# A hybrid layer on one core: rounded parts of x kept in DRAM between two sweeps, gates written as tanh, two transposes issued together, gates placed later

## The chip, the cores and the metric

One Trainium2 chip, one of its cores. The metric is the device time of one execution in microseconds (us), as the median of several runs. The core has five engines that work beside each other: PE (TensorE, matrix products), DVE (VectorE), ACT (ScalarE, functions from tables), POOL (GpSimd) and SP (SyncE, which here does nothing but issue DMAs). Each takes its instructions in its own order and waits on semaphores for the others.

## The reference

The function is one layer over a prompt of 2048 tokens and 8 decode sequences of 4 tokens, with model width 1024. Cut to what matters here:

```python
xn = rms_norm(x, g_mix_norm)
h  = xn @ w_in                        # widths: pool 256, rnn 512 + gate 512, attention 256
xc = causal_dwconv(rnn part)          # 4 taps
r  = sigmoid(xc @ w_rg_a + b_rg_a)    # 8 blocks of 64 x 64
i  = sigmoid(xc @ w_rg_x + b_rg_x)
log_a = -8 * r * softplus(-lam);  a = exp(log_a)
bt = sqrt(-expm1(2 * log_a)) * i * xc
h_t = a_t * h_{t-1} + bt_t            # scan over tokens
rnn_out = h * gelu(gate part)
pool_out: trailing means over 2, 4, 8, 16 tokens, minus the token, times w_pool
attn_out: cross attention, 4 heads of 64, over 256 memory rows (decode: its own cached k and v)
x = x + concat(group rms of the three) @ w_out
x = x + (gelu(conv3(xn2 @ w_ff_gate)) * (xn2 @ w_ff_up)) @ w_ff_down
y = rms_norm(x, g_final)
```

## The kernel before

Tokens stand on the columns, channels on the 128 partitions. The 2080 columns are cut into six slices s = 0 to 5 of 344 or 348 columns; slice 0 holds the 32 decode columns. All matrix products of the projections are made in rounded float32: an operand z is split into a high part, rounded by ACT, and a low part, z minus the high part, made by DVE (`split_g` does it for x with the norm's gain, L127 and L128), and a product is the sum of three matmuls (high times high, low times high, high times low). The two parts of two of x's eight chunks lie in a pair of tiles (`ahr`, `alr` in sweep 1, `ahp`, `alp` in sweep 2).

- Sweep 1 (0 to about 251 us of the profile) makes the recurrent branch. For each slice, `proj2` makes four groups of 48 matmuls: `pr` twice (the recurrent input) and `pq` twice (the gate input). DVE multiplies by the row norms (xr, L520; g, L549), ACT and DVE make the convolution (xc, L529 and L532), the block matrices give the gates (`g_gates`: pg on PE, L452; sigmoids on ACT, L455; the factor on DVE, L458), then ACT makes tanh (L466), exp (L469), the square (L470) and a square root (L472), which with DVE's L471 and L473 give the scan's input; L559 scans, L576 multiplies with gelu's result (L556).
- Then the keys and values of the memory, and sweep 2 (from about 263 us): the columns' x is loaded and split a second time (`xp`), and the pool and query projections (`pf` for slice 0, then `pq`), attention and pool are made. In the decode part, `pTd` holds two transposes of the softmax's result, L736, and `wz` its copies, L739; `pVd` (L745) multiplies with the cached values.
- Then the output projection, and three blocks of the feed-forward part (from about 525 us to the end).

What sets the order: PE and SP take their instructions in the order of the program's text. `Weave` holds generators (a norm, the gates, the preparation of the next slice) which are advanced between the matmuls of `proj2` when an estimated clock has passed their due time; the table `W` holds those waits. ACT, DVE and POOL are ordered by a scheduler when the program is built. A weight `w` is loaded to one of three staging tiles (`st_wr`) and split to `h_wr` and `l_wr` (L122, L123); the order of SP's loads decides when that starts. ACT loads a table of functions when the next function is not in the one it has (ACT_TABLE_LOAD).

Of the kernel before, what the change touches and what calls it, by code (L numbers as in the profile page):

```python
# [43 lines left out]
def hybrid_kernel(ctx: ExitStack, tc: tile.TileContext, I, O):  # L44
# [71 lines left out]
    def pcol(name, j):  # L116
        return pv[:, PC[name] + j:PC[name] + j + 1]


    def split(hi, lo, src, eng=None):  # L120

        S.activation(out=hi, in_=src, func=AF.Copy)  # L122
        (eng or V).tensor_tensor(out=lo, in0=src, in1=hi.bitcast(F32), op=ALU.subtract)  # L123

    def split_g(hi, lo, src, g):

        S.activation(out=hi, in_=src, func=AF.Copy, scale=g)  # L127
        V.scalar_tensor_tensor(out=lo, in0=src, scalar=g, in1=hi.bitcast(F32), op0=ALU.mult, op1=ALU.subtract)  # L128
# [106 lines left out]
    def half(h):  # L235
        return slice(64 * (h % 2), 64 * (h % 2) + 64)
# [4 lines left out]
    def psC(name):  # L241
        return ps.tile([P, 512], F32, tag="C", bufs=4, name=name)

    def g_prep(st, src, n, g, name, parts=2, wait=1.2, pool=0):

        x = big([P, 8, n], "x" + name)
        st += [x, [pair(f"{name}{k}", n) for k in range(KD // 2)]]
        w = KD // parts
        for k in range(KD):
            if k == 0 or (parts > 2 and k % w == 0):  # L250
                for h in range(k, k + w if parts > 2 else KD, w):
                    nc.sync.dma_start(out=x[:, h:h + w, :], in_=src[:, h:h + w, :])
            hi, lo = (z[:, k % 2, :] for z in st[1][k // 2])
            if k % 2 and k // 2 < pool:
                S.activation(out=x[:, k, :], in_=x[:, k, :], func=AF.Copy, scale=pcol(g, k))
                split(hi, lo, x[:, k, :], G)
            else:
                split_g(hi, lo, x[:, k, :], pcol(g, k))
# [186 lines left out]
    def g_gates(s, c2, n, st):  # L445

        xc, r, ii = st["xc"], st["r"], st["i"]
        dec = s == 0
        for c in (2 * c2, 2 * c2 + 1):
            pg = [psC(f"pg{s}{c}{h}") for h in range(2)]  # L450
            for h in range(2):
                T.matmul(pg[h][:, 0:n], bdg[half(h), c, :], xc[half(h), c, :], start=True, stop=True)  # L452
            for d, (dst, bias) in enumerate(((r, "ba"), (ii, "bx"))):
                for h in range(2):
                    S.activation(out=dst[half(h), c, :], in_=pg[h][half(d ^ h), 0:n], func=AF.Sigmoid,  # L455
                                 bias=pcol(bias, c)[half(h)])
            if c % 2:
                V.tensor_tensor(out=ii[:, c - 1:c + 1, :], in0=ii[:, c - 1:c + 1, :], in1=xc[:, c - 1:c + 1, :],  # L458
                                op=ALU.mult)
            yield 0.6, W["g2"]  # L460
        if c2 == 1:
            th = xc
            a2 = big([P, 4, n], f"a2{s}")

            for c in range(4):
                S.activation(out=th[:, c, :], in_=r[:, c, :], func=AF.Tanh, scale=sc8[:, c:c + 1])  # L466
            a = st["a"] = r
            for c in range(4):
                S.activation(out=a[:, c, :], in_=r[:, c, :], func=AF.Exp, scale=nl[:, c:c + 1])  # L469
            S.activation(out=a2, in_=a, func=AF.Square)  # L470
            V.scalar_tensor_tensor(out=th, in0=a2, scalar=1.0, in1=th, op0=ALU.add, op1=ALU.mult)  # L471
            S.activation(out=th, in_=th, func=AF.Sqrt)  # L472
            V.tensor_tensor(out=ii, in0=ii, in1=th, op=ALU.mult)  # L473
            if dec:
                d0 = kp.tile([P, 4, NB], F32, name="d0")
                V.tensor_tensor(out=d0, in0=t0(a), in1=h0, op=ALU.mult)
                V.tensor_tensor(out=t0(ii), in0=t0(ii), in1=d0, op=ALU.add)
                V.memset(t0(a), 0.0)

    for s in range(NS):  # L480
# [73 lines left out]
        while "a" not in st:
            wv.tick(0.5)
        S.activation(out=g, in_=g, func=AF.Gelu_apprx_tanh)  # L556
# [78 lines left out]
    def g_attn(s, n, npr, p0, qd, qs):  # L635
# [25 lines left out]
        def transp(j):  # L661
            e, c0, w = es[j]
            e_done.append(e)
            for mc in range(2):
                pT = psC(f"pT{s}{j}{mc}")
                for h in range(4):
                    T.transpose(pT[:, h * w:(h + 1) * w], e[:w, h, mc * P:(mc + 1) * P], ident[:w, :w])
                pv4 = pT[:, 0:4 * w].rearrange("p (h t) -> p h t", h=4)
                if mc >= W["n_pt"]:
                    S.activation(out=PT[:, mc, :, c0:c0 + w], in_=pv4, func=AF.Copy)  # L670
                else:
                    V.tensor_copy(PT[:, mc, :, c0:c0 + w], pv4)
# [33 lines left out]
    def g_dec(qd, ox):  # L706
# [27 lines left out]
        pT = psC("pTd")  # L734
        for mc in range(2):
            T.transpose(pT[:, mc * P:(mc + 1) * P], e[:, 0, mc * P:(mc + 1) * P], ident)  # L736
            pt4 = pT[:, mc * P:(mc + 1) * P].rearrange("p (g b m) -> p g b m", g=4, b=2)
            for b2 in range(2):
                V.tensor_copy(wf[:, mc, :, b2, 16 * b2:16 * b2 + 16], pt4[:, :, b2])  # L739
# [20 lines left out]
    for s in range(NS):  # L760
# [3 lines left out]
        p0 = ND if dec else 0  # L764
        npr = n - p0
        if s:
            wv.finish(pg_)
            x = xq.pop(s)
        rb = RBP.pop(s)
        if s + 1 < NS:  # L770
            xq[s + 1] = []
            pg_ = g_prep(xq[s + 1], x_src(s + 1), NCOL[s + 1], "g_mix", f"p{s + 1}", 2, W["prep_p"], W["n_prep"])
            wv.add(pg_)
            wv.tick(0.0)
        if s + 1 < NS:
            wv.add(g_bcast(rsx[:, s + 1, :], NCOL[s + 1], *TOK[s + 1], new_rbp(s + 1), f"p{s + 1}"), 0.0 if dec else W["bc_p"])
            wv.tick(0.0)
# [840 lines left out]
```

## Time and profile before

| | |
|---|---|
| median of 3 runs | 2127.59 us (2126.03 to 2129.19) |
| profiled execution | 2129.87 us, span 2128.0 us |
| PE busy | 2065.4 us, 97% |
| DVE busy | 1633.5 us, 77% |
| ACT busy | 1323.1 us, 62% |
| HBM read, written | 289.17 MB, 122.92 MB |

The span is what the trace covers; the execution's own time is 1.9 us more. A wait row names the waiting engine and tile, then the engine, tile and line whose end it waited for. A timeline row is start, duration, engine, line, operation, output from input, and in brackets how long the engine stood idle before. Where PE is at its full clock, a matmul of 348 columns follows the one before after 0.158 us; at half clock after about 0.29 us.

### The profile page before, as it was taken

To read this page: it belongs to the slowest core of one execution; us is meant where nothing else is said; L and a number is where in the kernel's file an instruction comes from. 1 tells how busy PE (TensorE), PEld (TensorE's weight loads), DVE (VectorE), ACT (ScalarE), POOL (GpSimd) and SP (SyncE) were. 2 spreads that over 40 slices of the span, in tenths; PEclk is the share of its full clock that TensorE was granted. 3 is DMA by queue.
4 is the path that set the end of the run, shared out by engine and by line. 5 is a ranking of instruction groups with operands and counts; after the bars stand their busy time and mean duration, and the time that the engine had idled before them with its cause. 6 is when DMAs were issued, how large, how long until landed. Compare 5 with 4: busy or idle time off the path is not lost.

```text
span 2128.0 us, 35270 instructions
## 1 busy us (share of the span) xinstructions
PE 2065.4 (97%) x12996; PEld 2009.0 (94%) x12996; DVE 1633.5 (77%) x2846; ACT 1323.1 (62%) x2380; POOL 69.3 (3%) x82
## 2 busy tenths in 40 slices
PE   8999998998999999999999999999999999999997
PEld 7888887888999999999999999999999999999997
DVE  7886897874878988889888666668778666668774
ACT  7879954552566656566655665557666665557663
POOL 0000000000000000000000000000000000000001
PEclk9999999999999999999999999999999999999998
DMA  4112342235997656677997555677887554677882
GB/s 144 55 55 90 126 169 85 66 111 199 286 305 232 229 194 217 197 242 219 260 262 230 188 187 162 211 261 223 245 248 186 190 191 158 217 261 221 247 226 86
DMA packets 257804, 408.72 MB, mean 192 GB/s; under 512 B 24416, under 2 KB 123456, under 8 KB 257632
## 3 DMA queue, kind: packets, MB, share of 16 engines
q1 hardware_dynamic: 242640, 367.19, 52.7%
q0 software_dynamic: 13760, 37.77, 8.4%
q8 instruction: 102, 1.67, 0.3%
q10 hardware_dynamic: 1232, 1.51, 0.2%
q14 instruction: 70, 0.57, 0.1%
HBM read 289.17 MB, written 122.92 MB: 194 GB/s over the span
## 4 chain that ended last, share of the span: by engine, by line
PE 80%; DVE 7%; ACT 5%; DMA 5%; issue 2%; SPq 0%; POOL 0%; POOLq 0%; DVEq 0%; ACTq 0%
PE bu L1054 9%; PE bg L1054 9%; PE bd L1054 9%; PE ag L1054 6%; PE cg L1054 6%; PE ad L1054 6%; PE cu L1054 6%; PE au L1054 6%; PE cd L1054 6%; PE pq L227 3%; PE po L227 2%; PE pu L227 2%; PE pr L227 1%; PE pf L227 1%; ACT r L455 1%
## 5 line engine op out<-in xcount | busy, mean ns | idle before, releaser
L1158 DVE SCALAR_TENSOR_TENSOR cv<-gt,pv,cv 128x696 f32<-128x696 f32 (+2 forms) x144 | 133.0, 924 | 34.9 <-ACT cv L1153 34.9
L1174 DVE TENSOR_TENSOR u<-u,cv 128x696 f32<-128x696 f32 (+1 forms) x72 | 63.3, 879 | 62.7 <-ACT cv L1170 62.7
L1220 POOL DMA_DIRECT2D ys<-cd x32 | 35.0, 1138 | 1367.2 <-ACT cd L1083 894.1
L1054 PE MATMUL bd<-h4s,wt4d 128*128 128x348 f32 (+1 forms) x288 | 72.8, 326 | 4.2 <-DVE cd L1076 4.2
L1054 PE MATMUL ag<-h5s,wt5g 128*128 128x348 f32 (+1 forms) x288 | 74.8, 322 | 0.0
L1054 PE MATMUL bg<-h4s,wt4g 128*128 128x348 f32 (+1 forms) x288 | 74.6, 322 | 0.0
L1054 PE MATMUL bg<-h1s,wt1g 128*128 128x348 f32 (+1 forms) x288 | 74.5, 322 | 0.0
L1054 PE MATMUL bg<-h3s,wt3g 128*128 128x348 f32 (+1 forms) x288 | 74.5, 322 | 0.0
L1054 PE MATMUL cu<-h6s,wt6u 128*128 128x348 f32 (+1 forms) x288 | 74.5, 321 | 0.0
L1054 PE MATMUL ag<-h0s,wt0g 128*128 128x348 f32 (+1 forms) x288 | 74.5, 321 | 0.0
L1054 PE MATMUL cg<-h6s,wt6g 128*128 128x348 f32 (+1 forms) x288 | 74.5, 321 | 0.0
L1054 PE MATMUL bu<-h4s,wt4u 128*128 128x348 f32 (+1 forms) x288 | 74.4, 321 | 0.1
L1054 PE MATMUL cg<-h2s,wt2g 128*128 128x348 f32 (+1 forms) x288 | 74.4, 321 | 0.0
L1054 PE MATMUL au<-h5s,wt5u 128*128 128x348 f32 (+1 forms) x288 | 74.4, 320 | 0.0
L1054 PE MATMUL au<-h0s,wt0u 128*128 128x348 f32 (+1 forms) x288 | 74.4, 320 | 0.0
L1054 PE MATMUL cu<-h2s,wt2u 128*128 128x348 f32 (+1 forms) x288 | 74.4, 320 | 0.0
L1054 PE MATMUL bu<-h1s,wt1u 128*128 128x348 f32 (+1 forms) x288 | 74.3, 321 | 0.0
L1054 PE MATMUL bu<-h3s,wt3u 128*128 128x348 f32 (+1 forms) x288 | 74.3, 321 | 0.0
L1054 PE MATMUL bd<-h3s,wt3d 128*128 128x348 f32 (+1 forms) x288 | 71.9, 322 | 2.1 <-ACT t6d L1072 2.1
L1054 PE MATMUL cd<-h6s,wt6d 128*128 128x348 f32 (+1 forms) x288 | 73.4, 326 | 0.0
L227 PE MATMUL pr<-ahr,h_wr 128*128 128x348 f32 (+1 forms) x192 | 64.8, 338 | 8.5 <-ACT ahr L127 8.5
L1054 PE MATMUL ad<-h0s,wt0d 128*128 128x348 f32 (+1 forms) x288 | 71.5, 321 | 0.0
(552 smaller groups left out, 7549.3 us busy)
## 6 DMA issues: line engine op xcount, KB each, us to landing
hs<-u SPq DMA_DIRECT2D x24, 696.0 KB, 4.1
ys<-cd POOLq DMA_DIRECT2D x20, 696.0 KB, 11.3
wr22g<-in_w_gate_dram SPq DMA_DIRECT2D x36, 256.0 KB, 4.1
wr11g<-in_w_gate_dram SPq DMA_DIRECT2D x36, 256.0 KB, 4.6
wr12g<-in_w_gate_dram SPq DMA_DIRECT2D x36, 256.0 KB, 4.7
wr22u<-in_w_up_dram SPq DMA_DIRECT2D x36, 256.0 KB, 6.5
wr11u<-in_w_up_dram SPq DMA_DIRECT2D x36, 256.0 KB, 6.6
wr12u<-in_w_up_dram SPq DMA_DIRECT2D x36, 256.0 KB, 6.2
```

The lines of the kernel that those rows point to most:

```text
L227: T.matmul(o, w_[:, ks], z, start=(k == 0 and i == 0), stop=(k == nk - 1 and i == 2))
L455: S.activation(out=dst[half(h), c, :], in_=pg[h][half(d ^ h), 0:n], func=AF.Sigmoid, bias=pcol(bias, c)[half(h)])
L1054: T.matmul(pt[:, 0:n], w[:, w_, ks_(k)], blk.hl[i][a_][:, k, :], start=(i in (0, 2) and k == m == 0), stop=(k == 3 and m == 2), skip_group ...
L1158: V.scalar_tensor_tensor(out=cv[:, z0:nn], in0=gt[:, z0 + t:nn + t], scalar=pcol("fcw", 3 * f + t), in1=cv[:, z0:nn], op0=ALU.mult, op1=AL ...
L1174: V.tensor_tensor(out=u, in0=u, in1=k["cv"][:, i, 0:nn], op=ALU.mult)
L1220: at[N + 14 + 1 + s].append(lambda j=2 * d + s, k=ks[s]: G.dma_start(out=flat(ys[b][j]), in_=qv(k["c"], n), accum_op=ALU.add, max_dma_last ...
```

## The change

Four edits, and the removal of some settings that were zero:

1. `g_prep` gets `keep`. After each odd chunk of x in sweep 1, SP stores the high and the low tile of the pair (128 x 688 or 696) to a DRAM buffer `xhl[s]`, eight DMAs a slice. In sweep 2 `load_parts(s)` loads the eight tiles, in place of the load of x and the eight ACT and eight DVE splits a slice.
2. The sigmoids are written as 0.5 (1 + tanh(0.5 z)): ACT uses Tanh with scale 0.5 and a halved bias `gb`; the factors of a half go into DVE's product with (i + 1), into scale and bias of the tanh and exp behind, and into the root's scale of 0.25.
3. Both transposes of `pTd` are issued ahead of the copies of `wz`.
4. `W["gate"]` goes from 6.8 to 8.2 and `W["g2"]` from 0 to 1.4, so the gates' matmuls stand later between those of the projections.

```diff
-    W = dict(... gate=6.8, ... g2=0)
+    W = dict(... gate=8.2, ... g2=1.4)
...
+    xhl = [dr.tile([P, 2, 8, n], F32, name=f"xhl{s}") for s, n in enumerate(NCOL)]
...
-    def g_prep(st, src, n, g, name, parts=2, wait=1.2, pool=0):
+    def g_prep(st, src, n, g, name, parts=2, wait=1.2, keep=None):
...
+            split_g(hi, lo, x[:, k, :], pcol(g, k))
+            if k % 2 and keep is not None:
+                for i in range(2):
+                    nc.sync.dma_start(out=keep[:, i, k - 1:k + 1], in_=st[1][k // 2][i].bitcast(F32))
             yield 0.0, wait
+
+    def load_parts(s):
+
+        x = [pair(f"p{s}{k}", NCOL[s]) for k in range(KD // 2)]
+        for k in range(KD // 2):
+            for i in range(2):
+                nc.sync.dma_start(out=x[k][i].bitcast(F32), in_=xhl[s][:, i, 2 * k:2 * k + 2])
+        return [None, x]
...
-    for k, _ in enumerate(g_prep(xq[0], x_src(0), NCOL[0], "g_mix", "r0", 4)):
+    for k, _ in enumerate(g_prep(xq[0], x_src(0), NCOL[0], "g_mix", "r0", 4, keep=xhl[0])):
...
-                    S.activation(out=dst[half(h), c, :], in_=pg[h][half(d ^ h), 0:n], func=AF.Sigmoid,
-                                 bias=pcol(bias, c)[half(h)])
+                    S.activation(out=dst[half(h), c, :], in_=pg[h][half(d ^ h), 0:n], func=AF.Tanh, scale=0.5,
+                                 bias=gb[half(h), bias + c:bias + c + 1])
...
-                V.tensor_tensor(out=ii[:, c - 1:c + 1, :], in0=ii[:, c - 1:c + 1, :], in1=xc[:, c - 1:c + 1, :],
-                                op=ALU.mult)
+                V.scalar_tensor_tensor(out=ii[:, c - 1:c + 1, :], in0=ii[:, c - 1:c + 1, :], scalar=1.0,
+                                       in1=xc[:, c - 1:c + 1, :], op0=ALU.add, op1=ALU.mult)
...
-                S.activation(out=th[:, c, :], in_=r[:, c, :], func=AF.Tanh, scale=sc8[:, c:c + 1])
+                S.activation(out=th[:, c, :], in_=r[:, c, :], func=AF.Tanh, scale=sc8[:, c:c + 1],
+                             bias=sc8[:, c:c + 1])
...
-            S.activation(out=th, in_=th, func=AF.Sqrt)
+            S.activation(out=th, in_=th, func=AF.Sqrt, scale=0.25)
...
-            pg_ = g_prep(xq[s + 1], x_src(s + 1), NCOL[s + 1], "g_mix", f"r{s + 1}", 2, W["prep_r"])
+            pg_ = g_prep(xq[s + 1], x_src(s + 1), NCOL[s + 1], "g_mix", f"r{s + 1}", 2, W["prep_r"], xhl[s + 1])
...
-            gp = g_prep(xp, x_src(0), NCOL[0], "g_mix", "p0", 2)
...
-    for _ in gp:
-        pass
-    x = xp
+    x = load_parts(0)
...
         for mc in range(2):
             T.transpose(pT[:, mc * P:(mc + 1) * P], e[:, 0, mc * P:(mc + 1) * P], ident)
+        for mc in range(2):
             pt4 = pT[:, mc * P:(mc + 1) * P].rearrange("p (g b m) -> p g b m", g=4, b=2)
...
-            xq[s + 1] = []
-            pg_ = g_prep(xq[s + 1], x_src(s + 1), NCOL[s + 1], "g_mix", f"p{s + 1}", 2, W["prep_p"], W["n_prep"])
-            wv.add(pg_)
-            wv.tick(0.0)
+            xq[s + 1] = load_parts(s + 1)
```

SP at the start of the program, before. `xr` is x of slice 0, its first quarter and then (x3) the others; `st_wr` is a weight's staging tile, the first one (wr0) in two halves.

```order
L135 DMA st_wr_107<-in_w_in_dram 128x512
L252 DMA xr_113<-in_x_dram 128x688
L135 DMA st_wr_107<-in_w_in_dram 128x512
L252 DMA xr_113<-in_x_dram 128x688 x3
L135 DMA st_wr_166<-in_w_in_dram 128x1024
L135 DMA st_wr_172<-in_w_in_dram 128x1024
L135 DMA st_wr_178<-in_w_in_dram 128x1024
```

SP at the same place after; these rows begin with the second half of wr0 (the first half, the first quarter and its two stores stand ahead of it), and `xhl_81` is the DRAM buffer of slice 0.

```order
L135 DMA st_wr_113<-in_w_in_dram 128x512
L253 DMA xr_119<-in_x_dram 128x688
L258 DMA xhl_81<-ahr_122 128x688
L258 DMA xhl_81<-alr_123 128x688
L253 DMA xr_119<-in_x_dram 128x688
L258 DMA xhl_81<-ahr_124 128x688
L258 DMA xhl_81<-alr_125 128x688
L253 DMA xr_119<-in_x_dram 128x688
L258 DMA xhl_81<-ahr_126 128x688
L258 DMA xhl_81<-alr_127 128x688
L135 DMA st_wr_182<-in_w_in_dram 128x1024
L135 DMA st_wr_188<-in_w_in_dram 128x1024
```

Each quarter's two stores now stand ahead of the next quarter's load, and all of them ahead of the second weight's.

ACT at the end of slice 2 in sweep 1, before, from the last gate's sigmoids (L455) to gelu (L556).

```order
L455 ACTIVATE i_988<-pg_1239,pv 64x348
L455 ACTIVATE i_988<-pg_1240,pv 64x348
L299 ACTIVATE rbr_1251<-bcr_1252 128x348
L469 ACT_TABLE_LOAD
L469 ACTIVATE r_987<-r_987,sp 128x348
L466 ACTIVATE xc_986<-r_987,sc_163 128x348 x2
L469 ACTIVATE r_987<-r_987,sp 128x348 x3
L470 ACTIVATE a_1260<-r_987 128x1392
L472 ACT_TABLE_LOAD
L472 ACTIVATE xc_986<-xc_986 128x1392
L556 ACT_TABLE_LOAD
L556 ACTIVATE g_1157<-g_1157 128x1392
```

The same place after; L465 are the gates' tanh, L480 exp, L482 the square, L484 the root, L565 gelu.

```order
L465 ACTIVATE i_1020<-pg_1290,gb 64x348
L465 ACTIVATE i_1020<-pg_1291,gb 64x348
L480 ACT_TABLE_LOAD
L480 ACTIVATE r_1019<-r_1019,sp 128x348
L476 ACTIVATE xc_1018<-r_1019,sc_177 128x348 x2
L480 ACTIVATE r_1019<-r_1019,sp 128x348 x3
L482 ACTIVATE a_1311<-r_1019 128x1392
L565 ACT_TABLE_LOAD
L565 ACTIVATE g_1183<-g_1183 128x1392
L484 ACT_TABLE_LOAD
L484 ACTIVATE xc_1018<-xc_1018 128x1392
```

Gelu with its table load stands ahead of the root here and in slice 4; in slices 1 and 3 the load at L480 is gone and the root stands first.

PE at the seam of the second `pr` group and the first `pq` group of slice 3, before; pg are the first gate's two matmuls, str those of a norm.

```order
L227 MATMUL pr_1423<-alr_981,h_wr_179 128x348
L227 MATMUL pr_1423<-ahr_980,l_wr_180 128x348
L452 MATMUL pg_1486<-xc_1354,bdg 128x348
L452 MATMUL pg_1487<-xc_1354,bdg 128x348
L227 MATMUL pr_1423<-ahr_980,h_wr_179 128x348
```

And after:

```order
L160 MATMUL str_1531<-ones,sqr_1401 116x1 x3
L228 MATMUL pq_1560<-ahr_1006,h_wr_211 128x348
L228 MATMUL pq_1560<-alr_1007,h_wr_211 128x348
L228 MATMUL pq_1560<-ahr_1006,l_wr_212 128x348
L462 MATMUL pg_1564<-xc_1394,bdg 128x348
L462 MATMUL pg_1565<-xc_1394,bdg 128x348
L228 MATMUL pq_1560<-ahr_1006,h_wr_211 128x348
```

The first gate of slice 3 moves from behind the 45th matmul of `pr` to behind the third of `pq`. The others of that slice stood behind the 3rd, 39th and 42nd of `pq`; now they stand behind the 15th and the 42nd, and the last behind the third of the second `pq` group.

More of the change, by code (lines that the diff above doesn't have):

```diff
@@ L54, in hybrid_kernel @@
     ctx.enter_context(tc.manual_schedule(engines={mybir.EngineType.SP}))
-    W = dict(pool_0=12.8, attn_0=1.42, soft0_0=9.0, st_p0=18.9, st_x5=13.5, n_prep=0, n_pt=0, n_q=0, n_wkv=0, n_wq=0,
-             norm_0=9.35, stat_0=2.55, prep_m=2.07, kv=11.0, gate=6.8, norm=14.0, stat=8.5, prep_r=9.7, mix_r=10.2,
-             sq_r=1.6, st_r=22.5, mix_5=14.0, sq_5=1.4, st_5=7.0, prep_p=3.0, bc_p=1.0, attn=0.42, soft0=8.5,
+    W = dict(pool_0=12.8, attn_0=1.42, soft0_0=9.0, st_p0=18.9, st_x5=13.5,
+             norm_0=9.35, stat_0=2.55, prep_m=2.07, kv=11.0, gate=8.2, norm=14.0, stat=8.5, prep_r=9.7, mix_r=10.2,
+             sq_r=1.6, st_r=22.5, mix_5=14.0, sq_5=1.4, st_5=7.0, bc_p=1.0, attn=0.42, soft0=8.5,
              soft1=2.0, soft2=8.5, pv=2.94, pool=10.3, sq_p=1.23, st_p=13.5, sq_x=1.16, st_x=10.5, dq=6.65,
-             dsoft=5.95, dpv=7.01, dout=1.5, mix0=1.19, g2=0)
+             dsoft=5.95, dpv=7.01, dout=1.5, mix0=1.19, g2=1.4)
     class Weave:
@@ L253, in g_prep @@
             hi, lo = (z[:, k % 2, :] for z in st[1][k // 2])
[L254 to L258, printed above, removed]
-            yield 0.0, wait
+            split_g(hi, lo, x[:, k, :], pcol(g, k))
+            if k % 2 and keep is not None:
+                for i in range(2):
+                    nc.sync.dma_start(out=keep[:, i, k - 1:k + 1], in_=st[1][k // 2][i].bitcast(F32))
+            yield 0.0, wait
+    def load_parts(s):
[4 more added lines that the diff above has]
+        return [None, x]
     def prep(*args):
@@ L420, in hybrid_kernel @@
     V.scalar_tensor_tensor(out=pp, in0=pp, scalar=1.0, in1=zz, op0=ALU.add, op1=ALU.mult)
-    V.tensor_scalar(out=nl, in0=nl, scalar1=0.0, scalar2=8.0, op0=ALU.max, op1=ALU.mult)
+    V.tensor_scalar(out=nl, in0=nl, scalar1=0.0, scalar2=4.0, op0=ALU.max, op1=ALU.mult)
     sc8 = cp.tile([P, 4], F32, name="sc8")
-    V.scalar_tensor_tensor(out=sc8, in0=pp, scalar=16.0, in1=nl, op0=ALU.mult, op1=ALU.add)
+    gb = cp.tile([P, 8], F32, name="gb")
+    V.tensor_scalar(out=gb, in0=pv[:, PC["ba"]:PC["ba"] + 8], scalar1=0.5, scalar2=None, op0=ALU.mult)
+    V.scalar_tensor_tensor(out=sc8, in0=pp, scalar=8.0, in1=nl, op0=ALU.mult, op1=ALU.add)
     V.tensor_scalar(out=nl, in0=sc8, scalar1=-1.0, scalar2=None, op0=ALU.mult)
@@ L452, in g_gates @@
                 T.matmul(pg[h][:, 0:n], bdg[half(h), c, :], xc[half(h), c, :], start=True, stop=True)
-            for d, (dst, bias) in enumerate(((r, "ba"), (ii, "bx"))):
+            for d, (dst, bias) in enumerate(((r, 0), (ii, 4))):
                 for h in range(2):
-                    S.activation(out=dst[half(h), c, :], in_=pg[h][half(d ^ h), 0:n], func=AF.Sigmoid,
-                                 bias=pcol(bias, c)[half(h)])
+                    S.activation(out=dst[half(h), c, :], in_=pg[h][half(d ^ h), 0:n], func=AF.Tanh, scale=0.5,
+                                 bias=gb[half(h), bias + c:bias + c + 1])
             if c % 2:
-                V.tensor_tensor(out=ii[:, c - 1:c + 1, :], in0=ii[:, c - 1:c + 1, :], in1=xc[:, c - 1:c + 1, :],
-                                op=ALU.mult)
+                V.scalar_tensor_tensor(out=ii[:, c - 1:c + 1, :], in0=ii[:, c - 1:c + 1, :], scalar=1.0,
+                                       in1=xc[:, c - 1:c + 1, :], op0=ALU.add, op1=ALU.mult)
             yield 0.6, W["g2"]
@@ L465, in g_gates @@
             for c in range(4):
-                S.activation(out=th[:, c, :], in_=r[:, c, :], func=AF.Tanh, scale=sc8[:, c:c + 1])
+                S.activation(out=th[:, c, :], in_=r[:, c, :], func=AF.Tanh, scale=sc8[:, c:c + 1],
+                             bias=sc8[:, c:c + 1])
             a = st["a"] = r
             for c in range(4):
-                S.activation(out=a[:, c, :], in_=r[:, c, :], func=AF.Exp, scale=nl[:, c:c + 1])
+                S.activation(out=a[:, c, :], in_=r[:, c, :], func=AF.Exp, scale=nl[:, c:c + 1],
+                             bias=nl[:, c:c + 1])
             S.activation(out=a2, in_=a, func=AF.Square)
             V.scalar_tensor_tensor(out=th, in0=a2, scalar=1.0, in1=th, op0=ALU.add, op1=ALU.mult)
-            S.activation(out=th, in_=th, func=AF.Sqrt)
+            S.activation(out=th, in_=th, func=AF.Sqrt, scale=0.25)
             V.tensor_tensor(out=ii, in0=ii, in1=th, op=ALU.mult)
@@ L495, in hybrid_kernel @@
         else:
-            wq, wkv, xm, xp = [], [], [], []
+            wq, wkv, xm = [], [], []
             pg_ = g_mem(xm)
@@ L544, in hybrid_kernel @@
             if s == NS - 1:
-                wkv += [load_w(I["wkv"][:, i * 1024:(i + 1) * 1024], f"wkv{i}", G if i % 2 < W["n_wkv"] else V) for i in (2 * c2, 2 * c2 + 1)]
+                wkv += [load_w(I["wkv"][:, i * 1024:(i + 1) * 1024], f"wkv{i}") for i in (2 * c2, 2 * c2 + 1)]
         g = tmp("t", [P, 4, n], f"g{s}")
@@ L550, in hybrid_kernel @@
             if s == NS - 1:
-                wq += [load_w(I["w_in"][c], f"wq{c}", G if c % 2 < W["n_wq"] else V) for c in ((10, 11), (0, 1))[c2]]
-                if c2 == 0:
-                    next(gp)
+                wq += [load_w(I["w_in"][c], f"wq{c}") for c in ((10, 11), (0, 1))[c2]]
         while "a" not in st:
@@ L668, in transp @@
                 pv4 = pT[:, 0:4 * w].rearrange("p (h t) -> p h t", h=4)
[L669 to L672, printed above, removed]
+                S.activation(out=PT[:, mc, :, c0:c0 + w], in_=pv4, func=AF.Copy)
         yield from g_room()
@@ L766, in hybrid_kernel @@
         if s:
-            wv.finish(pg_)
             x = xq.pop(s)
@@ L788, in hybrid_kernel @@
         qs = qs_[:, 0], qs_[:, 1]
-        split(*qs, q[:, :, p0:n], G if W["n_q"] else V)
+        split(*qs, q[:, :, p0:n])
         df = q[:, :, 0:n]
```

## The prediction

> **What bounds the kernel now.** I read the page first (busy shares, chain), then TensorE's waits over the whole span, then the timeline around each long wait, then stretches of a few microseconds for the granted clock.
>
> ```profile
> PE 2065.4 (97%) x12996; PEld 2009.0 (94%) x12996; DVE 1633.5 (77%) x2846; ACT 1323.1 (62%) x2380; POOL 69.3 (3%) x82
> ...
> PE 80%; DVE 7%; ACT 5%; DMA 5%; issue 2%; SPq 0%; POOL 0%; POOLq 0%; DVEq 0%; ACTq 0%
> ```
>
> TensorE (PE) is busy for 97% of 2128.0 us, and none of its matmuls in the projections is taken away. So an instruction removed on ScalarE (ACT) or VectorE (DVE) is worth nothing by itself; what can be won or lost is PE's 63 us of idle time, and the time at half clock behind an idle stretch. The waits name the places (us in total, times, longest):
>
> ```profile
> PE pr L227 <- ACT ahr L127: 8.5, 2, 5.4
> PE pTd L736 <- DVE wz L739: 5.1, 1, 5.1
> ...
> PE pf L227 <- DVE alp L128: 3.2, 2, 2.4
> PE pg L452 <- DVE xc L532: 3.2, 4, 1.1
> ```
>
> Of pr's 8.5, 5.4 is the very start and 3.1 stands at the second slice. The next rows give, per stretch, PE's busy time, then the other engines, then the clock granted to PE (PEclk, the third number from the end).
>
> ```profile
> 20.00:28.00 8.00, 6.97 (x45) 6.48 (x45) 7.54 (x21) 4.04 (x6) 0.00 (x0) 1.00 0.59 218
> 36.00:44.00 8.00, 7.00 (x32) 4.46 (x33) 8.00 (x16) 7.73 (x15) 0.00 (x0) 1.00 0.00 1
> 52.00:64.00 12.00, 7.96 (x36) 7.40 (x35) 8.20 (x17) 8.80 (x11) 0.00 (x0) 0.72 0.34 119
> 148.00:156.00 8.00, 7.77 (x35) 6.51 (x34) 8.00 (x26) 5.19 (x10) 0.72 (x1) 0.79 0.25 89
> 188.00:196.00 8.00, 8.00 (x30) 6.22 (x29) 7.67 (x23) 7.35 (x13) 0.71 (x1) 0.57 0.25 89
> 240.00:248.00 8.00, 8.00 (x33) 7.04 (x31) 5.00 (x15) 7.82 (x13) 0.56 (x1) 0.62 0.01 3
> 264.00:276.00 12.00, 8.77 (x41) 8.09 (x40) 12.00 (x21) 8.16 (x17) 2.32 (x4) 0.72 1.01 371
> 348.00:352.00 4.00, 3.43 (x15) 3.22 (x15) 1.84 (x7) 1.09 (x2) 0.00 (x0) 0.57 0.00 0
> ```
>
> Time lost to the clock is busy time by (1 - clock): 2.2 us in 52:64, 1.6, 3.4 and 3.0 us behind the gate stalls of slices 3, 4 and 5, 2.5 us in 264:276, 1.5 us in 348:352. The stall that starts such a stretch may be short: 1.01 us ahead of 188:196.
>
> ```profile
> 145.62 0.82 PE L452 MATMUL pg<-xc,bdg 64*128 64x348 f32 x3 [0.59 <-DVE xc L532]
> ...
> 185.77 0.85 PE L452 MATMUL pg<-xc,bdg 64*128 64x348 f32 x4 [1.01 <-DVE xc L532]
> ```
>
> In sentences of its own: the Trainium skill (TensorE: Matmul & The Clock Gate, Part 1) has the clock drop after an idle window of about 3.4 us. By that rule alone stalls of 0.6 to 1.1 us would cost only themselves, and term C below would be smaller by its clock part. The rows disagree (0.57 behind 1.01 us idle), and they decide.
>
> **A, the start: stores in SP's queue.** The stores of the kept parts are issued by SyncE (SP) in hand order. Ahead of the second, third and fourth quarter of x, and of the second weight wr1, there now stand two stores, which wait for ACT's and DVE's split of the quarter before. What was a stream becomes a chain of round trips.
>
> ```profile
> 1.19 0.42 SPq L252 DMA_DIRECT2D xr<-in_x_dram  x1
> ...
> 3.56 4.07 SPq L135 DMA_DIRECT2D st_wr<-in_w_in_dram  x3
> ```
> ```profile
> 4.79 1.05 ACT L127 ACTIVATE ahr<-xr,pv 128x344 fp32r<-128x344 f32 x2 [0.24 <-DMA xr<-in_x_dram]
> ...
> 10.88 1.04 ACT L122 ACTIVATE h_wr<-st_wr 128x1024 fp32r<-128x1024 f32 x1
> ```
> ```profile
> 5.53 1.06 DVE L128 SCALAR_TENSOR_TENSOR alr<-xr,pv,ahr 128x344 fp32r<-128x344 f32 x2
> ...
> 11.95 1.23 DVE L123 TENSOR_TENSOR l_wr<-st_wr,h_wr 128x1024 fp32r<-128x1024 f32 x1
> ```
> ```profile
> 13.23 0.43 PE L227 MATMUL pr<-ahr,l_wr 128*128 128x344 f32 x1 [0.33 <-DVE l_wr L123]
> ```
> ```profile
> st_wr<-in_w_in_dram SPq DMA_DIRECT2D x5, 512.0 KB, 5.6
> xr<-in_x_dram SPq DMA_DIRECT2D x4, 344.0 KB, 4.8
> ```
>
> A quarter lands 3.6 us after its issue (1.19 to 4.79), is split 1.8 us later (5.53 + 1.06 - 4.79), and the low part's store takes 0.42 us to issue, as the x load does: 5.9 us a trip with 0.1 for semaphores. Three more trips and the second half of wr0 (0.43) put the last quarter's landing at 22.9, wr1's issue at 25.2 instead of 3.56, its landing (3.7, hardly more than a quarter alone) at 28.9, and h_wr and l_wr (1.04, 1.23) at 31.2. PE needed l_wr of wr1 at 13.23: **+18.0**. With the median landings 4.8 and 5.6, taken while other loads were in flight, it is +23.6. I stay at the low end, since each load is now nearly alone. Restarting cold costs about +2.0 (between 1.5 and 2.5 above).
>
> Of this, some comes back in slice 0. From 20 to 28 and 36 to 44 PE idled 1.03 and 1.00 us for ACT and DVE, which have more lead now: -2.0. At the seam to slice 1 stands:
>
> ```profile
> PE pr L227 <- ACT ahr L127: 3.0, 1, 3.0
> ...
> PE pr L227 <- DVE alr L128: 1.0, 1, 1.0
> ```
>
> The last split of slice 1's x came behind the gelu and `a` on ACT; in the new order it stands ahead of the gates. These 4.0 us and their 2.2 of clock go: -6.2. ACT's tail then runs into slice 1's first gates; I put +1 there (0 to +4). A = 18.0 + 2.0 - 2.0 - 6.2 + 1.0 = **+12.8**, between +8 and +21. All other stores of sweep 1 stand behind work that is done a slice early, and queue 1 is idle there (DMA share 0.00 in 36:44): 0, bounded by +-1.
>
> **B, C, tanh and the gates' places.** A gate waits for the conv (xc), which waits on DVE for the scans of the slice before, those for ACT's tail:
>
> ```profile
> 124.58 1.28 ACT L469 ACT_TABLE_LOAD   x1
> ...
> 130.26 1.28 ACT L472 ACT_TABLE_LOAD   x1
> ...
> 133.30 1.28 ACT L556 ACT_TABLE_LOAD   x1
> 134.59 1.37 ACT L556 ACTIVATE g<-g 128x1392 f32<-128x1392 f32 x1
> ```
> ```profile
> 133.31 1.61 DVE L473 TENSOR_TENSOR i<-i,xc 128x1392 f32<-128x1392 f32 x1 [0.64 <-ACT xc L472]
> ```
>
> Moving the first gate six matmuls later, from the 45th of pr to the third of pq, gives 6 x 0.158 = 0.95 us of slack; alone it would cover 0.59 of slice 3, nearly all of 1.01 (slice 4) and of 1.06 (slice 5). But the last gates come 9 matmuls later too (1.4 us). In slices 1 and 3 the table load L469 goes and the tail ends about 1.1 us sooner. In slices 2 and 4 the new order keeps a load ahead of the exponentials and puts gelu with its load (1.28 + 1.37) ahead of the square root: `a` ends as before at 130.3, then come 1.28 + 1.37 (gelu), 1.28 + 1.37 (root) and DVE's 1.61, so L473 ends at 137.2 instead of 134.9, +2.3. So slice 4's stall goes (1.01 + 3.4 = -4.4); slice 5's shrinks a little against 0.95 to 1.4 of slack (-1); slice 3's grows by 1.4 or so, with some more half clock (+2.4). C = **-3**. If all the stalls go it is -(0.6 + 1.0 + 1.6 + 8.0) = -11; if slices 3 and 5 both take the whole 2.3 with a longer slow stretch, and slice 4 keeps its own, +6. The STT in place of the TT (L458), the scale and bias operands and `gb` add no instruction of note: 0.
>
> **D, the parts read back.** In sweep 2, 48 splits go on each engine:
>
> ```profile
> L127 ACT ACTIVATE ahp<-xp,pv x48: 563/580/616, 257.6 to 385.1; 128x348 fp32r<-128x348 f32 x32, 128x344 fp32r<-128x344 f32 x16
> ```
> ```profile
> L128 DVE SCALAR_TENSOR_TENSOR alp<-xp,pv,ahp x48: 549/571/583, 259.9 to 398.8; 128x348 fp32r<-128x348 f32 x32, 128x344 fp32r<-128x344 f32 x16
> ```
>
> 27.8 us of ACT and 27.4 us of DVE, on the path only where pf waits for them: 3.2 + 2.5 of clock = **-5.7** if slice 0's eight loads land before pf. Their buffers come free as sweep 1's last projection ends, near 251, pf starts near 264; 2.8 MB at 371 GB/s (264:276) are 7.6 us, so 4 us are left. The other slices' loads have 30 us. If they land late: 0. With the splits' cover gone, what is late next is the caches and the pool's constants, now behind eight more loads.
>
> **E, both transposes first.** The second pTd waited 5.1 us for copies that stood on DVE behind the pool's sums:
>
> ```profile
> 346.38 1.76 DVE L822 SCALAR_TENSOR_TENSOR qu<-wab,invw,qu 64x348 f32<-64x348 f32 x3
> 348.16 0.36 DVE L739 COPY wz<-pTd 128x64 f32<-128x64 f32 x2
> ```
> ```profile
> L745 PE MATMUL pVd<-vc,wz x32: 379/379/403, 356.9 to 358.5; 128*32 128x256 f32 x32
> ```
>
> The matmuls behind it move up; the next user, pVd, was at 356.9, would be at about 350.3, and the copies end by 349.9 at the latest, sooner without the splits between. So 5.1 + 1.5 = **-6.6**; -4 if pVd then waits. F, the small softmax waits of sweep 2, gain a little from emptier engines: **-1.8**, 0 to -3.5. The three FFN blocks are untouched: 0.
>
> **Sum:** 12.8 - 3.0 - 5.7 - 6.6 - 1.8 = -4.3, against the profiled execution (2129.87, with a span of 2128.0 and 1.9 around it) 2125.6. The median of the three runs, 2127.59, lies 2.3 lower, so 2123.3.
>
> **Rivals.** Gates clear altogether: the ordered tail is not on the path because DVE, freed elsewhere, takes the conv first; C = -11, so -12.3, 2115.3. For it: the stalls are only 0.6 to 1.1 us. Against: the +2.3 in slices 2 and 4.
>
> The other side: the start is dearer. If the stores slow the loads beside them, so that each lands as in the rows with 4.8 and 5.6, A is +18.4 and the sum +1.3, 2128.9; it gets slower than the bound from +21.4, when the loads land about 1 us later still (2133 at +22). For it: landings in the trace scatter. Against: 344 KB stores last about a microsecond at 371 GB/s.
>
> Also slower: the gelu ahead of the root lengthens the stalls of slices 3 and 5 and slice 4 keeps its own, C = +6: +4.7, 2132.3. For it: the longer tail of slices 2 and 4. The sum turns slower than the bound from C = +5.6.
>
> The read-back does not do what it says: slice 0's parts land after 264, D = 0: +1.4, 2129.0. For it: these loads stand behind four weight loads on SP. Against: 4 us left.
>
> **Numbers.** A measurement of this kernel tells about 0.2%, 4.3 us, from no change. The sum as it stands has a chance of 0.46 (0.27 faster than the bound, 0.19 within); gates clear 0.22 (all faster); start dearer 0.13 (0.09 slower, 0.04 within); tail longer 0.12 (0.10 slower, 0.02 within); read-back late 0.07 (0.04 within, 0.02 slower, 0.01 faster). Faster 0.50, same 0.29, slower 0.21. The range reaches from the gates' case with the small terms at their best to the slower cases: 2111 to 2136; the likeliest case alone spans 2118 to 2128.
>
> **What the changed profile would show.** A: SP issues wr1 near 25, and PE's second weight starts near 31; if near 14, A is wrong. C: waits of pg for xc in slices 3 and 5 but none in 4. D: no wait of pf for a split. E: no gap between the two pTd. The forecast fails most easily by A, whose trips add up four times.

## The result, and the profile after

The changed kernel takes 2146.63 us (median of 4 runs, 2141.98 to 2149.23), the kernel before 2126.81 us (4 runs, 2124.23 to 2129.19): ratio 1.0085, 95% interval 1.0067 to 1.0102. It is slower by some 18 us where 4 us less was forecast, and outside the stated range. The profiled execution is the shortest of the four, 2141.98 us with a span of 2140.1, so its trace shows 12.1 us of the difference (2140.1 against 2128.0). Two executions below ran in a disturbed, slower state, the profiled one of stores0_late (2514.6 us, clock 0.747) and one of parts_ptd (4038.88 us), and are left out of medians and marks.

The page after has the busy line and, from part 4, the chain:

```profile
PE 2061.3 (96%) x12996; PEld 2005.2 (94%) x12996; DVE 1613.5 (75%) x2799; ACT 1291.0 (60%) x2321; POOL 69.2 (3%) x82
...
PE 83%; DVE 7%; ACT 4%; DMA 3%; issue 2%; SPq 0%; POOL 0%; POOLq 0%; ACTq 0%; DVEq 0%
```

ACT lost 32 us of work and DVE 20, as meant, while PE's idle time grew from 63 to 79 us. The waits of PE after:

```profile
PE pr L228 <- ACT ahr L127: 15.8, 4, 5.4
PE str L160 <- DVE sqr L343: 9.0, 3, 5.4
PE pg L462 <- DVE xc L543: 7.3, 4, 2.9
...
PE pr L228 <- ACT h_wr L122: 4.5, 1, 4.5
...
PE pS L659 <- ACT rbp L307: 2.1, 1, 2.1
```

The waits of pf for alp and of pTd for wz are gone. In their place: pr waits for ahr at the start four times, once for each quarter of x, where it waited once; str (the norm of the next slice) waits for sqr, which it never did before; pg waits more than twice as long (7.3 us, before 3.2); and pS waits for rbp.

Where PE begins a stage tells where the time went. First the timeline of before (slice 2, the first pq behind pf, the output projection), then of after (the same, with the first pf and pu as well).

```profile
92.00 0.33 PE L227 MATMUL pr<-ahr,h_wr 128*128 128x348 f32 x1
...
286.43 0.40 PE L227 MATMUL pq<-ahp,h_wq 128*128 128x344 f32 x1
...
437.77 0.40 PE L227 MATMUL po<-ahm,h_wo 128*128 128x344 f32 x1
```
```profile
111.96 0.32 PE L228 MATMUL pr<-ahr,h_wr 128*128 128x348 f32 x1
...
288.03 0.40 PE L228 MATMUL pf<-ahp,h_wq 128*128 128x344 f32 x1
...
304.89 0.40 PE L228 MATMUL pq<-ahp,h_wq 128*128 128x344 f32 x1
...
320.11 0.31 PE L228 MATMUL pu<-ahp,h_wq 128*128 128x344 f32 x1
...
451.78 0.40 PE L228 MATMUL po<-ahm,h_wo 128*128 128x344 f32 x1
```

The delay is +20.0 us at slice 2, +24.6 at pf (before 263.41), +18.5 at the first pq behind it, +22.6 at the first pu (before 297.49), +14.0 at po and +12.1 at the end.

The start is much as it was reckoned:

```profile
7.55 0.48 SPq L253 DMA_DIRECT2D xr<-in_x_dram  x1
12.21 0.33 SPq L258 DMA_DIRECT2D xhl<-ahr  x1
12.84 0.33 SPq L258 DMA_DIRECT2D xhl<-alr  x1
13.21 0.46 SPq L253 DMA_DIRECT2D xr<-in_x_dram  x1
...
24.31 0.32 SPq L258 DMA_DIRECT2D xhl<-alr  x1
24.68 1.51 SPq L135 DMA_DIRECT2D st_wr<-in_w_in_dram  x3
```
```profile
31.36 0.65 PE L228 MATMUL pr<-ahr,l_wr 128*128 128x344 f32 x1 [0.32 <-DVE l_wr L123]
```

A trip is 5.66 us (7.55 to 13.21; 5.9 was reckoned), wr1 is issued at 24.68 (25.2 was reckoned), its low part used at 31.36 (31.2).

### The profile page after: what moved, and what is told of

Its sections match the earlier page's. It is cut to its first block, busy times and chain, and to the rows that moved or that the text cites. A ratio compares the mean times of both kernels' runs of the same rounds, so it can differ in the third digit from the quotient of the medians.

```text
span 2140.1 us, 35295 instructions
## 1 busy us (share of the span) xinstructions
PE 2061.3 (96%) x12996; PEld 2005.2 (94%) x12996; DVE 1613.5 (75%) x2799; ACT 1291.0 (60%) x2321; POOL 69.2 (3%) x82
## 4 chain that ended last, share of the span: by engine, by line
PE 83%; DVE 7%; ACT 4%; DMA 3%; issue 2%; SPq 0%; POOL 0%; POOLq 0%; ACTq 0%; DVEq 0%
PE bg L1055 10%; PE bu L1055 10%; PE bd L1055 9%; PE ag L1055 6%; PE cg L1055 6%; PE cu L1055 6%; PE au L1055 6%; PE ad L1055 6%; PE cd L1055 6%; PE pq L228 4%; PE po L228 2%; PE bo L1055 2%; PE pu L228 1%; PE co L1055 1%; PE ao L1055 1%
## 6 DMA issues: line engine op xcount, KB each, us to landing
ys<-cd POOLq DMA_DIRECT2D x20, 696.0 KB, 11.4
```

## The experiments

Fifteen runs. Each ratio is to the kernel before, run on the same chip. "po" is where the output projection begins in the one profiled execution, against 437.77 before.

| kernel | median us | ratio, 95% interval | po |
|---|---|---|---|
| changed kernel | 2146.63 | 1.0085, 1.0067 to 1.0102 | +14.0 |
| stores_pool | 2125.38 | 0.9985, 0.9972 to 0.9998 | -4.8 |
| stores0_pool | 2125.67 | 0.9980, 0.9966 to 0.9994 | -4.1 |
| stores0_late | 2141.26 | 1.0055, 1.0033 to 1.0077 | - |
| stores0_late_2 | 2139.08 | 1.0048, 1.0033 to 1.0064 | +11.1 |
| sp_oldplaces | 2136.34 | 1.0033, 1.0018 to 1.0047 | +6.2 |
| only_tanh | 2123.12 | 0.9976, 0.9965 to 0.9987 | -10.3 |
| only_places | 2142.63 | 1.0066, 1.0053 to 1.0079 | +9.8 |
| only_g2 | 2139.67 | 1.0051, 1.0036 to 1.0066 | +5.8 |
| tanh_places_ptd | 2131.72 | 1.0009, 0.9993 to 1.0024 | -2.0 |
| only_ptd | 2119.20 | 0.9964, 0.9948 to 0.9981 | -7.7 |
| tanh_ptd | 2115.45 | 0.9945, 0.9932 to 0.9957 | -14.2 |
| pool_oldplaces | 2117.31 | 0.9953, 0.9941 to 0.9965 | -12.6 |
| parts_ptd | 2120.49 | 0.9970, 0.9959 to 0.9981 | -11.1 |
| consts_first | 2115.98 | 0.9934, 0.9913 to 0.9955 | -12.7 |
| consts_first_2 | 2113.70 | 0.9931, 0.9919 to 0.9944 | -12.8 |

### Which queue issues the stores

```diff
 # stores_pool: all 48 stores on POOL
-                    nc.sync.dma_start(out=keep[:, i, k - 1:k + 1], ...)
+                    G.dma_start(out=keep[:, i, k - 1:k + 1], ...)
 # stores0_pool: slice 0's eight on POOL (parts > 2 only there), 40 on SP
+                    (G if parts > 2 else nc.sync).dma_start(out=keep[:, i, k - 1:k + 1], ...)
```

> The whole change, with the 48 stores of the kept parts issued by POOL instead of SP; nothing else differs in the text. Theory 1 (the stores block SP's queue, at the start and before each later slice's x load): l_wr of the second weight is used near 14 us again instead of 31.4, the waits of str for sqr (9.0 us in three) and most of the waits of pg for xc (7.3 us) go, and the time falls by 20 to 32 us against the changed kernel, to 2113 to 2126. Theory 2 (the start is SP's, but the waits of slices 1 to 5 come from the tanh order of ACT and the gates' places): the start's 18 us come back, the str and pg waits stay at 12 us or more, and the time is 2127 to 2131. Theory 3 (17 MB written and read back are the cost): less than 6 us come back, 2140 or more.

> The whole change with slice 0's eight stores on POOL and the 40 of slices 1 to 5 left on SP. If the cost of SP's queue is the start's round trips alone, the second weight is used near 14 us and the time is that of the kernel with all stores on POOL, 2123 to 2128 (19 to 21 us less than the changed kernel). If the later stores on SP, which hold back the next slice's x load, cost as well, 2130 to 2137.

Moving all stores brings 21 us (2146.6 to 2125.4), moving slice 0's eight alone the same (2125.7). So SP's cost is the start's chain of round trips; the 40 later stores on SP, though they stand ahead of the next slice's x load, cost nothing that these runs can tell. But the waits in slices 1 to 5 stayed, although Theory 1 had them go. PE's waits in the profile of stores_pool:

```profile
PE str L160 <- DVE sqr L343: 8.7, 3, 5.3
PE pr L228 <- ACT ahr L127: 6.1, 1, 6.1
...
PE pg L462 <- DVE xc L543: 5.9, 3, 2.9
```

These str and pg waits are nearly those of the changed kernel (9.0 and 7.3). Theory 2 is right for them: they are not SP's. The time alone would have misled: 2125.4 lies in Theory 1's range and 1.6 us below Theory 2's.

Slice 0's stores can also stand on SP behind the weights:

```diff
+    for k in range(KD // 2):          # behind the loads of wr4 to wr7
+        for i in range(2):
+            nc.sync.dma_start(out=xhl[0][:, i, 2 * k:2 * k + 2], in_=xq[0][1][k][i].bitcast(F32))
```

> The whole change, with slice 0's eight stores issued by SP behind the loads of all eight weights; the stores of slices 1 to 5 stay where they are. Theory 1: the second weight is used near 14 us, the later x loads are still late, and str's waits for sqr stay near 9 us: 13 to 18 us less than the changed kernel, 2128 to 2133. Theory 2 gives the same here. Theory 3: 2143 or more.

> The whole change with slice 0's stores behind the weights on SP, again. The second weight is used near 14 us. If slice 1's x, loaded behind the eight stores, is what is late, PE waits 8 us or more in pr of slice 1 for ahr and alr, and the time is 2138 to 2143; if that wait is short, the cost lies in slices 2 to 5.

Both theories missed: 5 to 8 us came back, not 13 to 18. The second run, with the time and the wait that were expected of it, shows the start mended and the seam to slice 1 broken. PE's waits between 40 and 80 us:

```profile
PE pr L228 <- ACT ahr L127: 7.0, 2, 5.8
PE pr L228 <- DVE alr L128: 5.0, 4, 2.9
PE pg L465 <- ACT i L468: 3.5, 1, 3.5
```

Slice 1's x is loaded at 31.18 behind the eight stores (in the kernel before at 23.17), and on ACT its last four splits stand behind the gates, the exponentials and the root, at 64.76; pr of slice 1, begun at 55.60, waits for them. The same x load at 42.12 in the changed kernel was followed by no wait of pr, since everything before it was late too.

### Tanh and the places of the gates

```diff
 # only_places: W in the kernel before
-   gate=6.8, ... g2=0
+   gate=8.2, ... g2=1.4
 # only_g2: g2=1.4 alone; only_tanh: edit 2 of the change alone
 # tanh_places_ptd: edits 2, 3 and 4, no kept parts
```

> The kernel before with the tanh gates, the later gate places and both transposes first, without the kept parts (x is loaded and split twice as before). Theory 1: no wait of str for sqr, small waits of pg for xc, and a time of 2113 to 2120. Theory 2: str and pg wait 12 us or more in slices 1 to 5 as in the changed kernel, and the time is 2123 to 2130.

> The kernel before with the gates written as tanh, nothing else; the gates' places are the old ones. Theory P (the later places cost: they make the last gates late, and the order of ACT then puts gelu ahead of the root): no wait of str for sqr, the waits of pg for xc 0 to 5 us, time 2119 to 2128. Theory T (the tanh writing itself costs): str and pg wait 12 us or more, time 2130 or more.

> The kernel before with only the two waits of the gates raised (6.8 to 8.2 and 0 to 1.4), sigmoids kept. Theory P: waits of str for sqr and of pg for xc of 10 us or more together, time 2131 to 2140. Theory T: those waits fall below before's 3.2 us, time 2121 to 2128.

> The kernel before with only the wait between two gates raised from 0 to 1.4; the first gate's wait stays. If the spread of the gates is what puts the tail late, most of the 15 us of both together is here: 2134 to 2142. If the first gate's place is, 2126 to 2131.

The later places cost, the tanh gains. tanh_places_ptd, without the kept parts, has the waits of str and pg too (8.8 and 5.9 us), as Theory 2 said, at a time 1.7 us above its range. only_tanh is 5 us faster than before, although not free of new waits (str 4.0, pg 5.7; none and at most 5 were expected). only_places is 14 us slower (0.66%; 2.6 us above Theory P's range), with sigmoids, and shows the changed kernel's waits without the rest of the change:

```profile
PE str L160 <- DVE sqr L335: 8.1, 3, 5.6
PE pg L452 <- DVE xc L532: 7.1, 5, 2.9
```

The wait between two gates alone (only_g2) gives 11 of the 14, but in another form. PE's longest waits there, the start aside, are

```profile
PE pg L452 <- DVE xc L532: 11.6, 4, 7.0
```

with a single 7.0 us in slice 2 and no str wait: the two settings do not act as two separate prices (the first gate's wait was not run alone). Together tanh (-5.1), places (+14.0) and transposes (-7.7) sum to +1.2, and tanh_places_ptd, which has all three, measures +1.9, within its interval.

Does the old placing help the changed kernel as well?

```diff
 # pool_oldplaces: stores_pool with gate=6.8, g2=0
 # sp_oldplaces: the changed kernel with gate=6.8, g2=0
```

> The whole change with the stores on POOL and the gates at their old places: tanh, kept parts, both transposes first. Theory P: the time falls by 10 us or more against the same kernel with the new places (2125.4), to 2104 to 2114. Theory T: 2122 to 2128.

> The whole change with the stores on SP and the gates at their old places. If the costs of SP's stores and of the places add up, 2146.6 less 8 (as with the stores on POOL), 2136 to 2141. If the late x loads hide the places' cost or the other way round, 2142 or more, or 2133 or less.

By 8 us with the stores on POOL and by 10 us with them on SP; Theory P's size was a little high for the first, the sign is right, and the two costs add up within the intervals. The mechanism can be read at slice 3, on ACT, on DVE and then on PE. After:

```profile
144.19 1.12 ACT L465 ACTIVATE i<-pg,gb 64x348 f32<-64x348 f32 x2
145.33 1.28 ACT L480 ACT_TABLE_LOAD   x1
...
150.19 1.37 ACT L482 ACTIVATE a<-r 128x1392 f32<-128x1392 f32 x1
151.57 1.28 ACT L565 ACT_TABLE_LOAD   x1
...
154.25 1.28 ACT L484 ACT_TABLE_LOAD   x1
```
```profile
156.94 1.61 DVE L485 TENSOR_TENSOR i<-i,xc 128x1392 f32<-128x1392 f32 x1 [3.75 <-ACT xc L484]
...
158.96 3.44 DVE L568 TENSOR_TENSOR_SCAN xc<-r,hcar,i 128x348 f32<-128x348 f32 x4
162.32 1.58 DVE L353 TENSOR_TENSOR sqr<-sqr 128x1392 f32<-128x1392 f32 x1
```
```profile
167.65 0.74 PE L160 MATMUL str<-ones,sqr 128*116 128x1 f32 x6 [2.74 <-DVE sqr L343]
...
170.90 0.95 PE L462 MATMUL pg<-xc,bdg 64*128 64x348 f32 x2 [1.92 <-DVE xc L543]
```

Slice 3's pr begins at 149.15. The product L485 ends 9.4 us later; before it ended 5.2 later (134.92 against 129.74), in pool_oldplaces 5.7 (136.48 against 130.75). DVE stands idle for 3.75 us, and behind L485 and the scans stand both the sum of squares that str waits for and the conv that pg waits for.

### The transposes

> The kernel before with both transposes of pTd issued ahead of the copies, nothing else. All theories: the gap of 5.15 us between the transposes and the half clock behind it go, 5 to 7 us less than before, 2120 to 2122. If the gap only moves to pVd, 0 to 2 us less.

```profile
L740 DVE COPY wz<-pTd x4: 216/216/225, 347.3 to 347.7; 128x64 f32<-128x64 f32 x4
...
L736 PE MATMUL pTd<-ident,ed x2: 270/270/271, 342.3 to 342.4; 128*128 128x128 f32 x2
```

2119.2 us, 0.36% below before, and 0.8 us below the range that was expected. By the medians it is the largest single gain of the change, though the intervals of it and of tanh overlap, and at the po mark tanh's is larger (-10.3 against -7.7). Both transposes run back to back; the copies still wait for the pool's sums until 347.3, and nobody waits for them.

### The read-back

```diff
 # parts_ptd: the kernel before with edits 1 (stores on POOL) and 3
 # consts_first: pool_oldplaces, and in the loop of sweep 2, for s == 0, ahead of load_parts(1):
+            icnt = ...; nc.sync.dma_start(out=icnt, ...)
+            upd = ...;  nc.sync.dma_start(out=upd, ...)
+            bdp = ...;  nc.sync.dma_start(out=bdp, ...)
 # tanh_ptd: edits 2 and 3, x split twice as before
```

> The kernel before with the kept parts (stores on POOL) and both transposes first; sigmoids and old places. Both theories: the two gains of sweep 2 and nothing lost, 12 to 14 us less than before, 2113 to 2116; against the kernel with the transposes alone (2119.2) that is the read-back's 4 to 6 us. If the stores themselves cost sweep 1 time, 2117 or more.

> Tanh, kept parts with the stores on POOL, transposes first, old places (2117.3), and in it the three small loads of the pool's constants and state moved ahead of slice 1's parts on SP. Theory: pS waited 2.05 us for rbp because rbp's buffer is read by the pool's decode product (upd, L831), which DVE does late, its state being loaded behind eight parts; then the wait and the half clock behind it go, 3 to 5 us less, 2111 to 2115. Rival: rbp waits for something else, 2116 to 2119.

> The kernel before with the tanh gates and both transposes first, old places, x split twice as before (no kept parts). If the read-back is worth the 5.7 us of the prediction, this is 4 us or more slower than the same kernel with the read-back and the constants first (consts_first_2): 2118 to 2121. If sweep 1 pays for the stores what sweep 2 gains, the two are within 3 us: 2113 to 2117.

> consts_first again, for the comparison on the same chip: 2113 to 2118.

parts_ptd (0.9970) is no faster than the transposes alone (0.9964), where 4 to 6 us had been expected; its one traced execution, its fastest, is 3.3 us ahead at po. Its waits of pf for alp are gone (only_ptd has 3.4 us of them), but PE waits elsewhere instead, and only_ptd has 0.9 us there:

```profile
PE pS L655 <- ACT e L631: 5.1, 2, 4.2
```

The mechanism that was expected of consts_first came, its time less clearly. In the changed kernel pS waited for rbp; on ACT and on DVE the reason stands in

```profile
312.40 0.46 ACT L307 ACTIVATE rbp<-bcp 128x348 f32<-128x348 f32 x1 [4.22 <-DVE upd L831]
```
```profile
312.12 0.19 DVE L831 TENSOR_TENSOR upd<-pf,rbp 128x32 f32<-128x32 f32 x1
```

rbp's buffer is free only when the pool's decode product has read it, and that product came late in DVE's order, its state being loaded behind slice 1's eight parts. With the small loads ahead of them, DVE's order has it 14 rows earlier and the pS wait is gone from PE's waits (286 to 306 us of consts_first):

```profile
PE pP L615 <- ACT e L635: 0.4, 1, 0.4
PE pT L674 <- ACT e L635: 0.3, 1, 0.3
```

The median fell by 1.3 us against pool_oldplaces on another chip (2117.3, 2116.0), the ratio by 0.19% (0.9953, 0.9934); 3 to 5 us were expected, and the intervals overlap. In the traces the way from pf to po is 2.8 us shorter (161.1 against 163.9), but the po mark does not show it, since pf itself begins 2.8 us later (264.01 against 261.23). That delay is a slow clock behind slice 5's gates, ahead of the edit.

What the read-back as a whole is worth depends on the rest. stores_pool and tanh_places_ptd, on one chip, differ by the kept parts alone: 0.24% (0.9985, 1.0009; the intervals just overlap), with 3.5 us of pf's waits for alp in the slower one. tanh_ptd against consts_first_2, also on one chip, has 0.14% (0.9945, 0.9931), which the intervals do not tell from nothing. There the wait that the read-back removes was already small:

```profile
PE pf L227 <- DVE alp L128: 0.9, 1, 0.9
```

So with tanh at the old places most of the gain at pf is there without the read-back.

consts_first is the fastest kernel that ran, 0.9931 (0.9919 to 0.9944) of before; tanh_ptd, a far smaller edit, is next to it.

## Why the prediction was wrong

Every sign that the prediction named for the changed profile came: wr1 near 25 and its use near 31, waits of pg in slices 3 and 5 and none in 4, no wait of pf for a split, no gap at pTd. The time was wrong all the same, because none of these signs would have shown a new wait.

**A, the start (+12.8; measured +20.0 at slice 2).** The delay of wr1's use was right to 0.1 us: +18.1 (31.36 against 13.23). Two small errors cancel in that: the issue of wr1 came 0.5 us sooner than reckoned, and from there to its use it took 6.7 us and not 6.0. At slice 1's first pr the delay is +18.4 (67.14 against 48.70), so the restart's "+2.0" and the "-2.0" nearly cancelled, as forecast. The step that failed is the credit of "-6.2" for the seam to slice 1, with only "+1" for what comes behind it. The seam did close: by the end of slice 1's second pr group the delay is down to +11.4 (82.44 against 71.02). But at once PE met a wait that had run beside the old one:

```profile
88.16 0.71 PE L160 MATMUL str<-ones,sqr 128*116 128x1 f32 x3 [5.41 <-DVE sqr L343]
```
```profile
87.50 0.52 DVE L343 TENSOR_TENSOR sqr<-sqr 128x348 f32<-128x348 f32 x1
```

Before, the same two steps stood at

```profile
71.17 0.67 PE L160 MATMUL str<-ones,sqr 128*116 128x1 f32 x6
```
```profile
68.86 0.51 DVE L335 TENSOR_TENSOR sqr<-sqr 128x348 f32<-128x348 f32 x1
```

Counted from slice 1's first pr, DVE has the sum ready after 20.9 us (88.02 - 67.14), before after 20.7 (69.37 - 48.70): it is hardly later. Before, PE came for it after 22.5 us, held up at the seam; now it comes after 15.6 and waits. So no more than 1.6 us of the credit (22.5 - 20.9) could be had. Of the kernels whose seam has no stall, those with the late places wait 5.3 to 5.6 us in slice 1's str, those with tanh at the old places 2.5 to 4.0; where the stores are issued makes no difference. The wait also brings its own slow stretch (0.68 in 84:100), as the stalls of before did, and slice 1 ends up costing 1.5 us more than before:

```profile
84.00:100.00 16.00, 11.84 (x57) 9.86 (x58) 14.65 (x38) 8.98 (x15) 0.56 (x1) 0.68 0.24 92
```

And the credit, even if had, is not the stores': pr's wait at the seam is gone as well in stores_pool and in only_tanh, so it offsets nothing of what the stores cost.

**C, the gates (-3; measured +4.6 from slice 2 to pf).** The step "`a` ends as before at 130.3" failed: relative to the slice's pr, `a` ended 1.9 us later (151.56 - 149.15 = 2.4, before 0.5), since the last gate's ACT work, behind 9 matmuls more on PE, ended 1.8 us later (145.31 against 149.15; before 124.07 against 129.74). With the reckoned +2.3 for gelu ahead of the root that makes L485's +4.2. The prediction named the last gates' delay (1.4 us) and left it out of the tail. Second, only the wait of pg was reckoned; str, whose sum of squares DVE now does behind the scans, waited 2.74 us in slice 3 and 0.82 in slice 4, and slice 5's gates waited 2.9 and 2.1 us where 1.06 and 0.50 stood before, and there L485 ended 9.9 us after the slice's first pr, before 4.6. By slices the trace has -0.6 in slice 2, +4.3 in slice 3 (+2.4 was forecast), -3.6 in slice 4 (-4.4) and +4.4 from slice 5 to pf (-1). The rival "tail longer" with C = +6 and a chance of 0.12 came nearest; but slice 4's stall, which it kept, did go. Together with A, near the dear end of its own range (+8 to +21), it makes the loss.

**D, the read-back (-5.7).** At pf it measured -6.1 (+24.6 to +18.5). But 4.1 us went back within the next stage (+18.5 to +22.6), where PE waited 2.05 us in pS for rbp, with a lower clock behind it. The prediction came near it with "what is late next is the caches and the pool's constants" and put no price on it.

**E, the transposes (-6.6).** Right: the delay falls from +21.1 at 340.47 (the pq of slice 3) to +14.2 at 365.09, -6.9; alone -7.7 on the po mark and 8 us in the medians. **F (-1.8)** cannot be seen: +14.2 at 365.09 and +14.0 at po.

The sum at po by the trace: 20.0 + 4.6 - 6.1 + 4.1 - 1.5 - 6.9 - 0.2 = +14.0; the 1.5 came back in slice 1's pu stage, right behind the pS wait. From po to the end each engine runs as many instructions as before, and the trace has -1.9. The medians differ by more than the traces because the traced execution of before is 3.1 us above its median and that of after 4.7 below. Why executions of one kernel differ by that much stays open, since no other execution has a trace.

## What to carry to other kernels

A store that waits for a computation does not belong in the queue that issues the loads: the eight stores cost 0.3 us each to issue, and 21 us by what stood behind them. With all stores on POOL (busy for 3% of the span before), slice 0's first pq began some 2 us later than without any (28.93 in stores_pool, 26.68 in tanh_places_ptd), pf 0.3 us (267.81, 267.54). When instructions are moved later, price what the moved ones feed (here the whole tail to the next slice) and every consumer in the other engine's order, not only the one whose wait is in the list. When a wait is removed, ask when the next input in the same stage is ready, counted from the stage's start, before booking the gain: two waits that run beside each other go only together. And book a gain only to the edit that brings it: one that another edit brings already offsets nothing.

## What was not expected

The stretch behind po holds the same work in all these kernels, and it scatters: from PE's wait of co for wt2o (536.16 before, 552.01 after) to the end of the span it took 1591.8 us before, 1588.1 after, 1585.9 in parts_ptd (from 526.20) and 1593.3 in only_tanh (from 527.93). A difference of 3 us between two spans is no evidence. The place where a fixed stage begins leaves this scatter out, but it too is read from one execution.

In the changed kernel the stalls of slice 3, 2.74 and 1.92 us, came with a clock of 0.83 in their stretch,

```profile
160.00:180.00 20.00, 15.34 (x79) 12.81 (x79) 17.26 (x34) 12.18 (x21) 0.72 (x1) 0.83 0.33 126
```

so that 4.66 us of waiting cost another 2.6 us of busy time at the lower clock (15.34 x 0.17). Short stalls do not always do this. pool_oldplaces and consts_first_2 run slice 5 alike, with 2.1 us of waits of pg for xc in three; behind them the clock was full in the first and 0.73 in the second:

```profile
242.00:250.00 8.00, 8.00 (x51) 7.91 (x50) 5.81 (x14) 7.94 (x12) 0.24 (x1) 1.00 0.35 122
```
```profile
242.00:250.00 8.00, 8.00 (x39) 8.00 (x40) 5.40 (x14) 7.94 (x12) 0.15 (x1) 0.73 0.20 68
```

The lower clock accounts for the 2.6 us by which pf begins later in consts_first_2 (263.86 against 261.23). What decides between the two stays open.
